# Search steps on PSUM operands, a second raw buffer, and eight gate tiles ahead of attention

## The chip, the cores and the metric

The kernel runs on one core of a Trainium2 chip. The metric is the device time of one launch in microseconds. Engines: PE (TensorE, matrix products), DVE (VectorE), ACT (ScalarE), POOL (GpSimd), and SP, whose queue issues the DMA transfers here.

## What is computed

One layer of a streaming encoder on 1024 prompt frames and 64 sample frames, width 1024, all in float32: a half-step feed-forward block, a block with sparse attention and a convolution in parallel, a second half-step feed-forward block, and a final norm. The middle block, cut to what matters:

```python
z = rms(h) @ w_in                       # q, k, v, q_idx, k_idx, w_idx, conv input, gates
s = einsum('bqhd,bsd->bqhs', q_idx, k_idx)
score = einsum('bqh,bqhs->bqs', w_idx, relu(s))          # -inf beyond the end of the frame's chunk of 64
_, sel = top_k(score, min(256, L // 4))                  # each query keeps its best keys
attn = softmax attention over the selected keys (8 heads, 2 key/value heads)
conv_out = silu(layernorm(depthwise_conv(glu(conv_in)))) @ conv_w_out
g_a, g_c = split(sigmoid(gate + b_gate))
h = h + (g_a * (attn @ attn_w_out) + g_c * conv_out) @ w_out
```

The keys are not gathered: the kernel finds, for each query row, which keys are among the best, and writes a bias row of 0 (keep) or a huge negative number (drop) that is added to the logits.

## The kernel before

Products are in split precision: each float32 operand is cut into a rounded high part and a low remainder, and every product is three matmuls (L154 to L156: high x high, high x low, low x high). Weights come by DMA (L135, `raw<-wf`), ACT makes the high part (L136, `whi`) and POOL the low part (L137, `wlo`).

The order on each engine is not written by hand. The program is traced in Python; a planner with a timeline simulation then orders the instructions of every engine at build time, by priority (a block of code can raise it; otherwise program order) and by when its model thinks operands are ready. On the chip each engine runs its own list strictly in that order. Buffers of a pool with a tag rotate: `bufs` copies exist, and a new use waits until the old one is free. When a pool is closed, later pools reuse its memory and wait for the tiles that lay there.

The stages around the change, in program order:

1. Indexer scores for seven query tiles (`STILES`: six of 128 rows with 384 to 1024 keys, and the sample tile of 64 rows with 192 keys) go into `Y` on DVE (L815). Its last head leaves row sums in `sums`; ACT's square (L817) leaves sums of squares in `cnt`.
2. Value projection, convolution inputs, and the rotated queries `d_q` (L595 to L600). The depthwise convolution runs meanwhile: ACT multiplies (L694, `pd`), POOL adds (L695, `ac`), 30 pairs for each half of a channel tile.
3. The search, all on DVE and with raised priority. Mean and spread of each row give a first threshold (L854 to L867, small steps on [128 x 7] tiles, one column for a query tile). Six rounds then count how many scores reach the threshold (L871, one pass for each query tile), with small steps between (L876 to L888) that move the threshold by a secant rule towards `goal`, top - 3.9. After the last count, L897 drops the counted keys from a copy `F` of the scores, L898 takes the eight largest remaining, `rank` (L891, L893) says how many of them are still needed, L899 and L900 remove these, and L904 writes the bias. L909 to L914 compare what was kept with what should be; if any row is off, a branch runs an exact but long search.
4. K (two groups, `load_k`, L715), V (L927) and the first query tile (`load_q`, L703) are loaded through a staging tile `raw2` in the pool `ak` (L715, L927, L703), and split by ACT (L170, L706) and DVE (L171, L707). `raw2` has one buffer. From the second on, the query tiles lie alternately in the attention pool `ap_`, whose memory follows that of the search's pool.
5. The gate projections: 16 tiles of 128 output columns, each for three column chunks of 362 or 364 frames: 48 groups of 24 matmuls. Each group is evicted by ACT (L942, `sg`) and stored (L943, `d_g`). The first `GPRE` tiles stand ahead of attention, with the four PSUM banks of the pool `ps4`; the others are the start of the "background".
6. Attention over nine query tiles in the order `TORD` = 8, 5, 6, 7, 4, 3, 2, 1, 0, four head pairs for each: logits (L989, L990) into three banks `lg`, bias and maximum on DVE (L992, `mb`), exponential on ACT (L1002), scaling on POOL and DVE (L1006), transposes (L1016) and the product with V. Between slots (pairs of key blocks) it calls the background `FILL[tile]` times; each call advances it by one step: a gate group, a step of the convolution's norm, of its output projection (L1123), of a merge (L1152, L1153) or of the output projection (L1165). A merge of a chunk is not traced before the attention of its frames.
7. The last merge and output projection, and the second feed-forward block.

The other four PSUM banks before attention belong to a pool `lgi`, used by the scores and by one convolution. Attention's pools take over the banks of both.

Of the kernel before, what the change touches and what calls it, by code (L numbers as in the profile page):

```python
# [20 lines left out]
P = 128  # L21
# [25 lines left out]
NLG, NPT = 3, 2  # L47
GPRE = 2
ROUNDS = 6
STOP = float(2 ** 126)  # L50
LOW = -1e36
MS = lambda nc: set()
FILL = {7: 1, 6: 1, 8: 4, 5: 1, 4: 1, 3: 2, 2: 2, 1: 2, 0: 2}
THI = 6000
# [41 lines left out]
def search_table():  # L96

    nd = NormalDist()
    t = np.zeros((P, 14, NT), np.float32)
    for n, (t0, rows, k0, L, top_) in enumerate(STILES):  # L100
        for half in range(2):
            r = slice(64 * half, 64 * half + 64)
            A = L - 64 * (1 - half) * (rows == P)
            z = nd.inv_cdf(1 - (top_ - 4) / A)
            t[r, 0, n], t[r, 1, n] = z, 1 / (A * nd.pdf(z))
        t[:, 2:6, n] = top_ - 3.9, top_, 1 / L, NEG * (L - top_)
    t[:, 6:] = np.tile(np.arange(8), NT).reshape(8, NT)
    return t.reshape(P, -1)


class Kern:
# [342 lines left out]
    def run(self):  # L454
        tc, nc, a = self.tc, self.nc, self.a
        PS = bass.MemoryType.PSUM
        with ExitStack() as top:
# [240 lines left out]
            def load_q(pool, src, t0, rows, qpool=None, qb=2, n=1280):  # L698

                raw = pool.tile([P, n], F32, name="raw2", tag="raw2")[:, 0:1024]  # L700
                raw = raw.rearrange("p (h c) -> p h c", h=8)[:, :, :rows]
                for i in range(4):
                    nc.sync.dma_start(raw[32 * i:32 * i + 32],  # L703
                                      src[i % 2, :, t0:t0 + rows].rearrange("(h r) c -> r h c", r=32))
                qt = (qpool or pool).tile([P, 8, P], F32R, name="qt", tag="qt", bufs=qb)[:, :, :rows]
                nc.scalar.activation(qt, raw, AF.Copy)  # L706
                nc.vector.tensor_tensor(qt[64:], raw[64:], qt[64:], op=ALU.subtract)  # L707
                return qt

            def load_k(pool, r0, name, tmp=None):  # L710
                kh = pool.tile([P, KCOLS], F32R, name=f"kh{name}")
                kl = pool.tile([P, KCOLS], F32R, name=f"kl{name}")
                raw = (tmp or pool).tile([P, 1280], F32, name="raw2", tag="raw2")[:, 0:KCOLS]
                for i in range(4):
                    nc.sync.dma_start(raw[32 * i:32 * i + 32, :], d_k[i % 2, r0:r0 + 32, :])  # L715
                self.split(kh, kl, raw)
                return kh, kl
# [43 lines left out]
            for i in (0, 1):  # L761
# [5 lines left out]
            small = lambda n, w=NT: kp.tile([P, w], F32, name=n)  # L767
            cnt, seen, exc, was, step, slope, gate, thr, unit = (
                small(n) for n in ("cnt", "seen", "exc", "was", "step", "slope", "gate", "thr", "unit"))
            sums = small("sums", 2 * NT)  # L770
            best = kp.tile([P, NT, 8], F32, name="best")
            rank = kp.tile([P, NT, 8], F32, name="rank")
            flags = kp.tile([P, 32], F32, name="flags")
# [9 lines left out]
            nc.sync.dma_start(zt, a["zt"])  # L783
            quant, inv, goal, wanted, per, expect = (zt[:, i * NT:(i + 1) * NT] for i in range(6))

# [10 lines left out]
            for n in SORD:  # L796
# [4 lines left out]
                for hd in range(8):  # L801
                    nb = 2 if L > 512 else 1
                    pw = L // nb
                    for b in range(nb):
# [8 lines left out]
                        else:  # L813
                            kw = {"accum_out": sums[:rows, 2 * n + b:2 * n + b + 1]} if hd == 7 else {}
                            nc.vector.scalar_tensor_tensor(yb, o, wrow[:, hd:hd + 1], yb,  # L815
                                                           op0=ALU.mult, op1=ALU.add, **kw)
                nc.scalar.activation(spare(n), y, AF.Square, accum_out=cnt[:rows, n:n + 1])  # L817
                if rows == P:
# [34 lines left out]
            v = nc.vector  # L853
            v.tensor_tensor(step, sums[:, 0:2 * NT:2], sums[:, 1:2 * NT:2], op=ALU.add)  # L854
            v.tensor_tensor(step, step, per, op=ALU.mult)
            v.tensor_tensor(cnt, cnt, per, op=ALU.mult)
            v.tensor_tensor(slope, step, step, op=ALU.mult)
            v.tensor_tensor(slope, cnt, slope, op=ALU.subtract)
            v.tensor_scalar(exc.bitcast(I32), slope.bitcast(I32), -0.5, 1597463007.0, op0=ALU.mult, op1=ALU.add)
            for i in range(2):  # L860
                v.tensor_tensor(gate, slope, exc, op=ALU.mult)
                v.scalar_tensor_tensor(gate, gate, -0.5, exc, op0=ALU.mult, op1=ALU.mult)
                v.scalar_tensor_tensor(exc, gate, 1.5, exc, op0=ALU.add, op1=ALU.mult)
            v.tensor_tensor(slope, slope, exc, op=ALU.mult)
            v.tensor_tensor(thr, slope, quant, op=ALU.mult)
            v.tensor_tensor(thr, thr, step, op=ALU.add)
            v.tensor_tensor(unit, slope, inv, op=ALU.mult)  # L867
            for r in range(ROUNDS):
                for n in range(NT):
                    rows, y0, L = rows_of(n)  # L870
                    v.tensor_scalar(spare(n), Y[:rows, y0:y0 + L], thr[:rows, n:n + 1], 0.0,  # L871
                                    op0=ALU.is_ge, op1=ALU.add, accum_out=cnt[:rows, n:n + 1])
                if r == ROUNDS - 1:
                    break
                exc, was = was, exc
                v.tensor_tensor(exc, cnt, goal, op=ALU.subtract)  # L876
                v.tensor_tensor(gate, exc, exc, op=ALU.mult)
                if r:
                    v.scalar_tensor_tensor(slope, was, 0.001, exc, op0=ALU.add, op1=ALU.subtract)
                    v.reciprocal(slope, slope)  # L880
                    v.tensor_tensor(slope, slope, step, op=ALU.mult)
                    v.tensor_scalar(slope, slope, 0.25, 4.0, op0=ALU.max, op1=ALU.min)
                    v.tensor_tensor(step, exc, slope, op=ALU.mult)
                else:
                    v.tensor_copy(step, exc)
                v.scalar_tensor_tensor(gate, gate, 16.9, step, op0=ALU.is_gt, op1=ALU.mult)
                v.tensor_tensor(gate, gate, unit, op=ALU.mult)
                v.tensor_tensor(thr, thr, gate, op=ALU.add)  # L888

            v.tensor_tensor(gate, wanted, cnt, op=ALU.subtract)  # L890
            v.tensor_tensor(rank, gate.rearrange("p (n o) -> p n o", o=1).to_broadcast([P, NT, 8]),  # L891
                            zt[:, 6 * NT:].rearrange("p (n o) -> p n o", o=8), op=ALU.is_gt)
            v.tensor_scalar(rank, rank, 2 * STOP, -STOP, op0=ALU.mult, op1=ALU.add)  # L893
            for n in range(NT):
                rows, y0, L = rows_of(n)
                f = F[:rows, y0:y0 + L]
                v.scalar_tensor_tensor(f, spare(n), -STOP, Y[:rows, y0:y0 + L], op0=ALU.mult, op1=ALU.add)  # L897
                v.max(best[:rows, n, :], f)  # L898
                v.tensor_tensor(best[:rows, n, :], best[:rows, n, :], rank[:rows, n, :], op=ALU.min)  # L899
# [25 lines left out]
            vt = ak.tile([P, 2, 10, P], F32R, name="vt")  # L925
            raw = ak.tile([P, 1280], F32, name="raw2", tag="raw2").rearrange("p (b d) -> p b d", d=P)
            nc.sync.dma_start(raw[:, 0:9, :], d_v[:, 0:9, :])  # L927
# [498 lines left out]
```

## Time and profile before

| | us |
|---|---|
| median of 3 runs | 2435.06 (2434.07 to 2438.32) |
| profiled execution | 2435.61 |
| its span | 2433.8 |
| PE busy | 2307.9 (95%) |
| DVE busy | 1677.8 (69%) |
| POOL busy | 1404.1 (58%) |
| ACT busy | 1146.8 (47%) |

The span is the time from the first to the last instruction that the profiler saw; the 1.8 us beside it lie around the program. Rows of the profile name an engine, a line of the kernel, the tile written and the tiles read. A row of waits reads: who waited, for whom, total us, times, longest. A row with a stretch reads: from and to in us, its length, then the busy time and number of instructions of each engine, the granted clock of PE (1.00 is full), the DMA share and GB/s. A row of a line reads: number, then shortest, median and longest duration in ns, first and last start.

### The profile page before, as it was taken

How to read it: one execution, taken by the hardware profiler on the slowest of the kernel's cores; microseconds unless marked ns; L12 is line 12 of the kernel's file. 1: busy time of each engine (PE TensorE's matmuls, PEld its weight loads, DVE VectorE, ACT ScalarE, POOL GpSimd, SP SyncE). 2: the span in 40 equal slices, each digit the busy share in tenths (PEclk: the TensorE clock that was granted, in tenths of full speed). 3: DMA queues.
4: the chain of work that ended last, by engine and by line, in shares of the span. 5: the costliest groups of instructions: out<-in, count | busy, mean ns of one | idle time of the engine just before them, and what ended most of it. 6: DMA issues, size and time to landing. Idle time of an engine off the chain costs nothing.

```text
span 2433.8 us, 43946 instructions
## 1 busy us (share of the span) xinstructions
PE 2307.9 (95%) x16762; PEld 2278.1 (94%) x16762; DVE 1677.8 (69%) x3600; ACT 1146.8 (47%) x2189; POOL 1404.1 (58%) x861
## 2 busy tenths in 40 slices
PE   5999999999999999989699888799999999999998
PEld 5999999999999999989699888799999999999997
DVE  7666678666678386689634897358666677776676
ACT  5434445434346556865554664235443445433343
POOL 4555555555557786888662444457555555555554
PEclk9999999999999999999899999899999999999999
DMA  4222223223224344333223345752232322332223
GB/s 164 96 96 96 93 99 122 98 88 105 96 90 137 126 136 126 95 113 100 63 83 110 102 143 173 261 175 101 87 105 87 100 99 80 110 104 102 96 96 116
DMA packets 130118, 271.92 MB, mean 112 GB/s; under 512 B 18032, under 2 KB 77296, under 8 KB 129904
## 3 DMA queue, kind: packets, MB, share of 16 engines
q1 hardware_dynamic: 129904, 269.08, 33.1%
q8 instruction: 132, 2.16, 0.4%
q14 instruction: 82, 0.67, 0.1%
HBM read 230.34 MB, written 38.75 MB: 111 GB/s over the span
## 4 chain that ended last, share of the span: by engine, by line
PE 40%; DVE 6%; DMA 3%; issue 1%; ACT 1%; POOL 0%; SPq 0%; DVEq 0%; ACTq 0%
PE ps L154 12%; PE ps L156 12%; PE ps L155 12%; DMA ga<-d_g 1%; PE pt L1016 1%; DVE ga L1153 1%; DMA d_mp<-gc 1%; PE lg L989 1%; PE lg L990 0%; PE ps L184 0%; DVE pr L992 0%; PE pv L154 0%; DMA hr<-d_h 0%; DMA gc<-d_g 0%; PE pv L155 0%
## 5 line engine op out<-in xcount | busy, mean ns | idle before, releaser
L137 POOL TENSOR_TENSOR wlo<-raw,whi 128x1024 fp32r<-128x1024 f32 (+1 forms) x187 | 435.4, 2333 | 421.9 <-ACT whi L136 406.7
L154 PE MATMUL ps<-x,wp 128*128 128x272 f32 x1760 | 508.8, 291 | 11.2 <-DVE spare L302 9.2
L156 PE MATMUL ps<-x,wp 128*128 128x272 f32 x1760 | 506.3, 291 | 1.0 <-DVE wp L171 0.4
L155 PE MATMUL ps<-x,wp 128*128 128x272 f32 x1760 | 506.9, 289 | 0.0
L154 PE MATMUL ps<-x,whi 128*128 128x272 f32 (+2 forms) x1544 | 483.2, 313 | 18.2 <-ACT sg L942 8.8
L156 PE MATMUL ps<-x,wlo 128*128 128x272 f32 (+2 forms) x1544 | 481.5, 312 | 0.0
L155 PE MATMUL ps<-x,whi 128*128 128x272 f32 (+2 forms) x1334 | 412.3, 309 | 0.0
L154 PE MATMUL ps<-gh,whi 128*128 128x272 f32 x1408 | 400.0, 289 | 6.8 <-DVE spare L302 5.0
L155 PE MATMUL ps<-gl,whi 128*128 128x272 f32 x1408 | 404.9, 289 | 0.0
L156 PE MATMUL ps<-gh,wlo 128*128 128x272 f32 x1408 | 403.8, 288 | 0.0
L171 POOL TENSOR_TENSOR wlo<-raw,whi 128x1024 fp32r<-128x1024 f32 x88 | 220.1, 2502 | 263.8 <-ACT whi L170 260.6
L154 PEld LDWEIGHTS ps<-x,wp 128*128 128x128 f32 x1760 | 333.1, 189 | 12.2 <-ACT wp L170 12.2
L155 PEld LDWEIGHTS ps<-x,wp 128*128 128x128 f32 x1760 | 333.6, 190 | 0.0
L156 PEld LDWEIGHTS ps<-x,wp 128*128 128x128 f32 x1760 | 331.0, 189 | 2.3 <-DVE wp L171 1.7
L154 PEld LDWEIGHTS ps<-x,whi 128*128 128x128 f32 x1544 | 293.1, 190 | 20.3 <-ACT sg L942 9.3
L171 POOL TENSOR_TENSOR wp<-s,wp 128x512 fp32r<-128x512 f32 x176 | 258.7, 1470 | 90.0 <-ACT wp L170 90.0
L136 ACT ACTIVATE whi<-raw 128x1024 fp32r<-128x1024 f32 (+1 forms) x187 | 190.7, 1020 | 234.8 <-PE ps L155 127.2
L156 PEld LDWEIGHTS ps<-x,wlo 128*128 128x128 f32 x1544 | 292.9, 190 | 1.0
L442 DVE SCALAR_TENSOR_TENSOR h<-ps,h 128x272 f32<-128x272 f32 x384 | 164.7, 439 | 184.7 <-PE ps L156 184.2
L695 POOL TENSOR_TENSOR ac<-ac,pd 128x559 f32<-128x559 f32 x180 | 259.8, 1444 | 45.8 <-ACT pd L694 15.5
L154 PEld LDWEIGHTS ps<-gh,whi 128*128 128x128 f32 x1408 | 263.0, 189 | 8.3 <-DVE spare L302 5.7
L156 PEld LDWEIGHTS ps<-gh,wlo 128*128 128x128 f32 x1408 | 265.8, 189 | 0.0
(236 smaller groups left out, 4815.3 us busy)
## 6 DMA issues: line engine op xcount, KB each, us to landing
raw<-wf SPq DMA_DIRECT2D x334, 512.0 KB, 3.2
raw<-wf SPq DMA_DIRECT2D x32, 384.0 KB, 3.0
d_g<-sg SPq DMA_DIRECT2D x32, 181.0 KB, 1.9
d_h<-h SPq DMA_DIRECT2D x2, 2176.0 KB, 10.4
y<-t SPq DMA_DIRECT2D x32, 136.0 KB, 1.8
raw<-d_q SPq DMA_DIRECT2D x32, 128.0 KB, 2.7
raw<-d_qi SPq DMA_DIRECT2D x24, 128.0 KB, 3.0
d_g<-sg SPq DMA_DIRECT2D x16, 182.0 KB, 2.0
```

What stands on the lines that cost most here:

```text
L136: nc.scalar.activation(hi[:, :n], raw[:, :n], AF.Copy)
L137: self.weng.tensor_tensor(lo[:, :n], raw[:, :n], hi[:, :n], op=ALU.subtract)
L154: t.matmul(out, wh, xh, start=first, stop=False)
L155: t.matmul(out, wh, xl, start=False, stop=False)
L156: t.matmul(out, wl, xh, start=False, stop=last)
L171: (eng or nc.vector).tensor_tensor(lo, x, hi, op=ALU.subtract)
L442: nc.vector.scalar_tensor_tensor(x, p, 0.5, x, op0=ALU.mult, op1=ALU.add)
L695: nc.gpsimd.tensor_tensor(ac, ac, pd, op=ALU.add)
L989: nc.tensor.matmul(o, q, kh[:, ks:ks + pw], start=True, stop=False)
L1016: nc.tensor.transpose(pt[:kn, o:o + r], u.pr[hh][:, kk:kk + kn], ident[:r, :r])
L1153: nc.vector.scalar_tensor_tensor(ga, mpt, 0.5, ga, op0=ALU.mult, op1=ALU.add)
```

## The change

- The search's small tiles: `goal`, `over`, `slope`, `gate`, `cen` and `rank` become slices of one PSUM bank (`bank`, from the pool `lgi`). `goal` is copied there from the table, `exc` is computed a second time as `over` in PSUM, the mean is held twice (`cen` in PSUM, `mean` in SBUF), and a root of its own (`root`) takes the place of `exc` in the square root. Most small steps then read at most one operand from SBUF.
- ACT's square is scaled by L to the power -0.5, so that the step that divided `cnt` goes.
- The rank table holds o - 3.4 rather than o, and is compared with `goal` - `cnt` rather than `wanted` - `cnt`. For whole counts both give the same answer.
- In the last round, count, L897's drop and L898's maximum are done tile by tile, and no longer all counts first.
- `raw2` in the pool `ak` has two buffers.
- `GPRE` is 8 rather than 2, and `FILL[8]` is 2 rather than 4.

```diff
-GPRE = 2
+GPRE = 8
-FILL = {7: 1, 6: 1, 8: 4, 5: 1, 4: 1, 3: 2, 2: 2, 1: 2, 0: 2}
+FILL = {7: 1, 6: 1, 8: 2, 5: 1, 4: 1, 3: 2, 2: 2, 1: 2, 0: 2}
-    t[:, 6:] = np.tile(np.arange(8), NT).reshape(8, NT)
+    t[:, 6:] = np.tile(np.arange(8) - 3.4, NT).reshape(8, NT)
...
-                raw = pool.tile([P, n], F32, name="raw2", tag="raw2")[:, 0:1024]
+                raw = pool.tile([P, n], F32, name="raw2", tag="raw2", bufs=2 if n == 1280 else 1)[:, 0:1024]
-                raw = (tmp or pool).tile([P, 1280], F32, name="raw2", tag="raw2")[:, 0:KCOLS]
+                raw = (tmp or pool).tile([P, 1280], F32, name="raw2", tag="raw2", bufs=1 if tmp else 2)[:, 0:KCOLS]
...
-                nc.scalar.activation(spare(n), y, AF.Square, accum_out=cnt[:rows, n:n + 1])
+                nc.scalar.activation(spare(n), y, AF.Square, scale=L ** -0.5, accum_out=cnt[:rows, n:n + 1])
...
-            v.tensor_tensor(step, sums[:, 0:2 * NT:2], sums[:, 1:2 * NT:2], op=ALU.add)
-            v.tensor_tensor(step, step, per, op=ALU.mult)
-            v.tensor_tensor(cnt, cnt, per, op=ALU.mult)
-            v.tensor_tensor(slope, step, step, op=ALU.mult)
+            bank = lgi.tile([P, 512], F32, name="srch", tag="lgi")
+            goal, over, slope, gate, cen = (bank[:, 16 * i:16 * i + NT] for i in range(5))
+            rank = bank[:, 128:128 + 8 * NT].rearrange("p (n o) -> p n o", o=8)
+            v.tensor_copy(goal, target)
+            v.tensor_tensor(gate, sums[:, 0:2 * NT:2], sums[:, 1:2 * NT:2], op=ALU.add)
+            v.tensor_tensor(cen, gate, per, op=ALU.mult)
+            v.tensor_tensor(mean, gate, per, op=ALU.mult)
+            v.tensor_tensor(slope, cen, mean, op=ALU.mult)
...
+            for r in range(ROUNDS - 1):
+                for n in range(NT):
+                    count(n, spare(n))
                 exc, was = was, exc
+                v.tensor_tensor(over, cnt, goal, op=ALU.subtract)
                 v.tensor_tensor(exc, cnt, goal, op=ALU.subtract)
-                v.tensor_tensor(gate, exc, exc, op=ALU.mult)
+                v.tensor_tensor(gate, exc, over, op=ALU.mult)
                 if r:
-                    v.scalar_tensor_tensor(slope, was, 0.001, exc, op0=ALU.add, op1=ALU.subtract)
+                    v.scalar_tensor_tensor(slope, was, 0.001, over, op0=ALU.add, op1=ALU.subtract)
...
-                    v.tensor_copy(step, exc)
+                    v.tensor_scalar(step, over, 1.0, None, op0=ALU.mult)
...
-            v.tensor_tensor(gate, wanted, cnt, op=ALU.subtract)
+            for n in range(NT):
+                rows, y0, L = rows_of(n)
+                f = F[:rows, y0:y0 + L]
+                count(n, spare(n))
+                v.scalar_tensor_tensor(f, spare(n), -STOP, Y[:rows, y0:y0 + L], op0=ALU.mult, op1=ALU.add)
+                v.max(best[:rows, n, :], f)
+            v.tensor_tensor(gate, goal, cnt, op=ALU.subtract)
...
-                v.scalar_tensor_tensor(f, spare(n), -STOP, Y[:rows, y0:y0 + L], op0=ALU.mult, op1=ALU.add)
-                v.max(best[:rows, n, :], f)
...
-            raw = ak.tile([P, 1280], F32, name="raw2", tag="raw2").rearrange("p (b d) -> p b d", d=P)
+            raw = ak.tile([P, 1280], F32, name="raw2", tag="raw2", bufs=2).rearrange("p (b d) -> p b d", d=P)
```

More of the change, by code (lines that the diff above doesn't have):

```diff
@@ L767, in run @@
             small = lambda n, w=NT: kp.tile([P, w], F32, name=n)
-            cnt, seen, exc, was, step, slope, gate, thr, unit = (
-                small(n) for n in ("cnt", "seen", "exc", "was", "step", "slope", "gate", "thr", "unit"))
+            cnt, seen, exc, was, step, mean, thr, unit, root = (
+                small(n) for n in ("cnt", "seen", "exc", "was", "step", "mean", "thr", "unit", "root"))
             sums = small("sums", 2 * NT)
             best = kp.tile([P, NT, 8], F32, name="best")
-            rank = kp.tile([P, NT, 8], F32, name="rank")
             flags = kp.tile([P, 32], F32, name="flags")
@@ L783, in run @@
             nc.sync.dma_start(zt, a["zt"])
-            quant, inv, goal, wanted, per, expect = (zt[:, i * NT:(i + 1) * NT] for i in range(6))
+            quant, inv, target, wanted, per, expect = (zt[:, i * NT:(i + 1) * NT] for i in range(6))
             def rows_of(n):
@@ L858, in run @@
+            v.tensor_copy(goal, target)
[3 more added lines that the diff above has]
+            v.tensor_tensor(slope, cen, mean, op=ALU.mult)
             v.tensor_tensor(slope, cnt, slope, op=ALU.subtract)
-            v.tensor_scalar(exc.bitcast(I32), slope.bitcast(I32), -0.5, 1597463007.0, op0=ALU.mult, op1=ALU.add)
+            v.tensor_scalar(root.bitcast(I32), slope.bitcast(I32), -0.5, 1597463007.0, op0=ALU.mult, op1=ALU.add)
@@ L860, in run @@
             for i in range(2):
[L861 to L864, printed above, removed]
+                v.tensor_tensor(gate, slope, root, op=ALU.mult)
+                v.scalar_tensor_tensor(gate, gate, -0.5, root, op0=ALU.mult, op1=ALU.mult)
+                v.scalar_tensor_tensor(root, gate, 1.5, root, op0=ALU.add, op1=ALU.mult)
@@ L865, in run, with count @@
+            v.tensor_tensor(slope, slope, root, op=ALU.mult)
             v.tensor_tensor(thr, slope, quant, op=ALU.mult)
-            v.tensor_tensor(thr, thr, step, op=ALU.add)
+            v.tensor_tensor(thr, thr, cen, op=ALU.add)
             v.tensor_tensor(unit, slope, inv, op=ALU.mult)
-            for r in range(ROUNDS):
-                for n in range(NT):
[L870 to L874, printed above, removed]
+            def count(n, out):
+                rows, y0, L = rows_of(n)
+                v.tensor_scalar(out, Y[:rows, y0:y0 + L], thr[:rows, n:n + 1], 0.0,
+                                op0=ALU.is_ge, op1=ALU.add, accum_out=cnt[:rows, n:n + 1])
@@ L888, in run @@
                 v.tensor_tensor(thr, thr, gate, op=ALU.add)
-            v.tensor_tensor(gate, wanted, cnt, op=ALU.subtract)
+            for n in range(NT):
+                rows, y0, L = rows_of(n)
+                f = F[:rows, y0:y0 + L]
[3 more added lines that the diff above has]
+            v.tensor_tensor(gate, goal, cnt, op=ALU.subtract)
             v.tensor_tensor(rank, gate.rearrange("p (n o) -> p n o", o=1).to_broadcast([P, NT, 8]),
```

## The prediction

> **What bounds the kernel now.** I read the profile's page first (shares and the forty slices), then busy time by stretches, then the waits of each engine around the stretch that stood out, then DVE's timeline inside it.
>
> ```profile
> span 2433.8 us, 43946 instructions
> PE 2307.9 (95%) x16762; PEld 2278.1 (94%) x16762; DVE 1677.8 (69%) x3600; ACT 1146.8 (47%) x2189; POOL 1404.1 (58%) x861
> ```
>
> PE is busy for 95% of the span, so a gain is PE idle time removed. The 126 us of it that are idle are not spread evenly:
>
> ```profile
> 1077.00:1088.00 11.00, 2.17 (x12) 1.87 (x11) 10.59 (x33) 5.92 (x8) 3.09 (x3) 0.69 0.71 206
> 1130.00:1153.00 23.00, 23.00 (x141) 23.00 (x140) 22.96 (x29) 10.34 (x15) 18.03 (x12) 1.00 0.35 113
> 1153.00:1174.00 21.00, 0.62 (x4) 0.31 (x3) 13.85 (x48) 0.81 (x1) 0.84 (x1) 0.58 0.00 0
> 1174.00:1320.00 146.00, 145.33 (x940) 140.40 (x940) 68.69 (x173) 83.91 (x163) 88.97 (x50) 0.99 0.27 86
> 1320.00:1487.00 167.00, 152.29 (x1037) 142.07 (x1035) 139.54 (x367) 99.71 (x223) 75.75 (x45) 0.97 0.43 131
> ```
>
> Columns: stretch, length, then busy time of PE, PEld, DVE, ACT, POOL, the granted clock, DMA share, GB/s. The key search runs on DVE from 1057 to 1173. PE covers it with gate projections, but has two holes: about 9 us near 1080 and 20 us before 1174. After 1174 PE is full (145.33 of 146), so time gained there is kept.
>
> ```profile
> PE lg L989 <- DVE mb L992: 21.1, 2, 20.4
> PE ps L154 <- ACT sg L942: 8.8, 1, 8.8
> ACT qt L706 <- DVEq L914: 22.3, 1, 22.3
> ACT kh L170 <- DMA raw<-d_k: 7.2, 1, 7.2
> SPq L703 <- DVE qt L707: 26.9, 1, 26.9
> 1153.10 0.33 PE L156 MATMUL ps<-x,wlo 128*128 128x364 f32 x1
> 1173.81 0.42 PE L989 MATMUL lg<-kh,qt 128*64 128x192 f32 x1 [20.38 <-DVE mb L992]
> L942 ACT ACTIVATE sg<-ps,hb x20: 542/564/567, 1058.9 to 1146.0; 128x362 f32<-128x362 f32 x13, 128x364 f32<-128x364 f32 x7
> ```
>
> (Total, times, longest.) The big hole: PE has a logit matmul next in its queue, waiting for DVE, and DVE is still in the search and its branch (L914). ACT stands 22.3 us at the second query tile's conversion, which waits for that branch, and SP stands 26.9 us behind the only raw buffer. Twenty gate groups were evicted and about two more computed when all stopped: although only two gate tiles (6 groups) stand ahead of attention in the program, the planner had already pulled 22 groups forward. A group is 24 matmuls; at 141 matmuls in 23 us that is 3.9 us, or 4.0 with the 364-frame chunks.
>
> **The change part by part.**
>
> *Small steps on PSUM.* Six stretches hold all small steps from the sums to the last threshold update:
>
> ```profile
> 1057.27:1066.38 9.11, 8.62 (x16) 1.00 0.62 187
> 1073.98:1077.47 3.49, 3.32 (x8) 1.00 0.60 177
> 1084.34:1086.24 1.90, 1.60 (x11) 0.50 0.56 124
> 1095.35:1100.41 5.06, 4.75 (x11) 1.00 0.39 108
> 1107.62:1115.05 7.43, 7.12 (x11) 1.00 0.68 189
> 1120.69:1130.19 9.50, 9.20 (x10) 1.00 0.13 44
> sum 36.49, DVE 34.60; mean DVE 5.77
> 1126.35 0.17 DVE L886 SCALAR_TENSOR_TENSOR gate<-gate,step 128x7 f32<-128x7 f32 x1
> 1126.55 1.25 DVE L887 TENSOR_TENSOR gate<-gate,unit 128x7 f32<-128x7 f32 x1
> 1127.84 2.32 DVE L888 TENSOR_TENSOR thr<-thr,gate 128x7 f32<-128x7 f32 x1
> L207 DVE TENSOR_TENSOR rt<-rv,ps x57: 145/157/159, 11.4 to 2425.1; 128x3 f32<-128x3 f32 x54, 128x4 f32<-128x4 f32 x3
> L208 DVE SCALAR_TENSOR_TENSOR rt<-rt,ps x57: 135/157/159, 11.9 to 2425.3; 128x3 f32<-128x3 f32 x54, 128x4 f32<-128x4 f32 x3
> ```
>
> The third round had POOL idle: ten steps in 1.90 us, 0.19 each. The last round, the same ten steps beside a busy POOL (7 adds and weight splits), took 9.50: 7-column steps of 0.17 become 1.25 or 2.32. The nearest rows with one operand in PSUM are the norm's steps, L207 and L208: 114 of them over the whole span, POOL 58% busy, none above 0.159. So I price every changed step at 0.20. Before there are 16 + 6 + 4x10 = 62 steps; after 17 + 7 + 4x11 = 68 (a copy of the goals, a second centre, `over` in each round; the square's scale removes one). 68 x 0.20 = 13.6 against 36.5. One new step, `gate` from two halves of the sums, still reads SBUF twice: +0.7, its excess now. Search shorter by 22.2 us; bounds 22.9 (no waits at all) and -1.2, that is longer, if PSUM does not help and only the six steps are added.
>
> *Rank table and reordered last round.* The same comparisons of integers with shifted constants, and the same 7 counts, 7 combinations (L897) and 7 maxima, interleaved: no instruction gone. The prices that matter are these:
>
> ```profile
> 1135.74:1148.85 13.11, 13.11 (x81) 13.11 (x80) 13.11 (x11) 6.42 (x10) 11.45 (x6) 1.00 0.37 116
> 1157.76:1165.57 7.81, 0.00 (x0) 0.00 (x0) 7.80 (x22) 0.00 (x0) 0.00 (x0) 0.50 0.00 0
> L904 DVE SCALAR_TENSOR_TENSOR bias<-F,fill x7: 345/814/1210, 1157.8 to 1165.2; 128x384 bf16<-128x384 f32 x1, 128x512 bf16<-128x512 f32 x1, 128x640 bf16<-128x640 f32 x1, 128x768 bf16<-128x768 f32 x1
> 1166.24 0.19 DVE L912 TENSOR_REDUCE flag<-turned 128x1 int32<-128x32 f32 x1
> 1173.40 0.35 DVE L992 CUSTOM_DVE_ANT_0 pr<-lg,bias 64x192 f32<-64x192 f32 x1 [6.98 <-DVEq L914]
> ```
>
> The combinations read two SBUF tiles and took 13.1 us beside a POOL busy for 11.45. The seven masks (L904) have the same shapes and also read two SBUF tiles, but took 0.81 in the middle, 5.6 in all, with POOL at 0.00 (late replacements fill the rest of the 7.81). POOL was idle there only because ACT was stuck and fed it nothing. Once the search ends sooner, some masks fall where POOL still works. From 0 to (13.1 - 5.6) = 7.5 us more; I take 3. The flag and the branch stay at 7 us. The search's end moves from 1173.1 to 1173.1 - 22.2 + 3 = 1153.9.
>
> The Trainium skill has a rule that speaks against this change here: "SBUF — State Buffer", section Who interferes with whom, says a DVE instruction with two SBUF inputs contends with a GpSimd instruction that reads SBUF, and the later one waits in full. By it all seven masks would wait wherever POOL is busy; the L897 row agrees, no run here shows it for masks. The sum by it is the second rival below.
>
> *Second raw buffer.* K's second group could not be loaded until DVE had split the first; ACT stood 7.2 us for it, and the eviction behind it, the sixth, held PE for 8.8:
>
> ```profile
> 1086.99 0.54 ACT L942 ACTIVATE sg<-ps,hb 128x362 f32<-128x362 f32 x1
> 1087.58 0.67 PE L154 MATMUL ps<-x,whi 128*128 128x364 f32 x1 [8.83 <-ACT sg L942]
> ```
>
> With two buffers the load is issued early. The 8.8 us do not add to the gain: without them the other 18 groups run from 1087.58 - 8.83 = 1078.7 and end at 1078.7 + 18 x 3.95 = 1149.8 rather than 1160, in either case near the search's end. Worth 0 to 2 by itself; if the cover (the search) were gone, 8.8. SP's 26.9 us go too; what is late next is the second query conversion, which still waits for the branch.
>
> *Eight gate tiles ahead, FILL[8] 4 to 2.* No matmul, transfer or eviction is added. Ahead of attention must now stand 24 groups, not the 22 that the planner had put there: 2 x 4.0 = 8.0 us of PE work moves into a hole. The price: attention's banks come from the gates' pool, so no logits are computed ahead, and the last evictions and the ninth tile's weights queue on ACT behind the query conversion. I bound this backlog from below by that conversion alone and from above by conversion, weight split, three evictions and some five conv products with POOL's pace:
>
> ```profile
> 1173.19 1.06 ACT L706 ACTIVATE qt<-raw 128x1024 fp32r<-128x1024 f32 x1 [22.33 <-DVEq L914]
> 1174.16 1.04 ACT L136 ACTIVATE whi<-raw 128x1024 fp32r<-128x1024 f32 x1
> 1175.10 0.55 ACT L942 ACTIVATE sg<-ps,hb 128x362 f32<-128x362 f32 x1
> L695 POOL TENSOR_TENSOR ac<-ac,pd x44: 1373/1392/2247, 1118.9 to 1249.4; 128x559 f32<-128x559 f32 x44
> ```
>
> 1 to 1.06 + 1.04 + 3 x 0.55 + 5 x 1.39 = 11 us; I take 6. PE resumes at 1153.9 + 6 = 1160, not 1173.8: 13.8 us.
>
> In the background's list, gates fall from 42 steps to 24; 78 others stay. Fill calls fall from 120 to 112, so ten find nothing, near tile 2, where the merge waits for attention. A conv-out step there is 12 matmuls, 2.0 us; ten make 20. The matmuls are only moved, so this costs PE idle at most: 0 to 20. At the 9% that PE is idle from 1320 to 1487, 2 us.
>
> **Sum.** -13.8 - 8.0 + 2 = -20 us. The profiled execution took 2435.61 (span 2433.8, 1.8 around it), 0.5 above the median of 2435.06. I apply -20 to the median: 2415.
>
> **The rivals.**
>
> 1. *The backlog takes the place of the search.* ACT's order, or the freeing of the gates' banks, holds the first logits 10 us longer than I allow. For: ACT's single 22.3 us wait held everything. Against: the planner puts evictions at PE's pace. -20 + 10: 2425.
> 2. *Masks wait for POOL.* 7.5 in place of 3: 2419.5. For: L897's row. Against: ACT stops feeding POOL when it reaches the query conversion.
> 3. *The steps still wait.* Then the search ends at 1174.3; only the two groups move, less 1.2 and 2 for the fills: -5, 2430. Against: L207, L208.
> 4. *Slower: attention runs out of filler.* Ten empty calls at tile 2, where PE then waits for DVE. At 2.0 us each it leaves 2 us of the gain, 2433; at the 4.0 us of an output-projection step (24 matmuls) it is +40 in place of +2: 2453. It decides from 2.2 us of new idle per empty call. Against: PE was idle for only 14.7 us in the whole of that stretch, and the planner fills from further down.
> 5. *Larger gain.* No mask waits (3), backlog of 1 (5), and the freed SP and the conv that runs on save some 5 more of the 14.7: -33, 2402.
>
> **How the numbers follow.** Chances: forecast 0.50 (its own range 2405 to 2423), rival 1 0.15, 2 0.12, 3 0.04, 4 0.11, 5 0.08. Low: rival 5 less a few us, 2399; high: rival 1 with some of 3, 2429. Rival 4's 0.11 stays mostly outside. About 0.2% (4.9 us) is what a measurement can tell from no change. Faster: 0.50 + 0.12 of rival 1 + 0.12 + 0.02 + 0.08 = 0.84. Same: 0.03 of rival 1, 0.02 of 3, 0.03 of 4 = 0.08. Slower: 0.08 of 4.
>
> **What would show it.** Steps right: none of the PSUM steps above 0.25, six stretches near 14 us in sum. Search: the branch ends near 1154. Gates: 24 evictions before the first logit, and PE's hole at most 12 us. Raw buffer: no wait of ACT for d_k near 1071, none of SP on L707 beyond a few us. Masks: their stretch at 8 to 15. Wrong would be: the hole still 20 us, steps above 1 us, or more than 25 us of PE idle in the 167 us after the dense stretch.

## The result, and the profile after

The changed kernel took 2394.70 us (median of 4 runs, 2393.04 to 2398.54) against 2435.23 for the kernel before (4 runs, 2434.07 to 2438.32): ratio 0.9834, 95% interval 0.9817 to 0.9851. That is 40.5 us where 20 were forecast, and below the range (2399). The profiled execution took 2394.04, its span 2392.3, 41.5 less than before. Lines have moved: the scores L815 are L814 in the changed kernel, the eviction L942 is now L952, the logits L989 and L990 are L999 and L1000, the masks L904 are L914, the flag L912 is L922, the branch L914 is L924, the merge's L1152 is L1162.

The page of the changed kernel, first line of engines:

```profile
PE 2301.7 (96%) x16762; PEld 2272.7 (95%) x16762; DVE 1656.9 (69%) x3606; ACT 1145.4 (48%) x2189; POOL 1410.0 (59%) x861
```

PE idle fell from 125.9 us (2433.8 - 2307.9) to 90.6. The other 6.2 us are busy time: the same 16762 matmuls took less. Where the idle went is read from four stretches. Kernel before:

```profile
1040.00:1160.00 120.00, 104.60 (x628) 103.77 (x626) 112.85 (x218) 64.88 (x102) 95.32 (x62) 0.94 0.34 106
1160.00:1290.00 130.00, 115.51 (x747) 111.48 (x748) 62.94 (x166) 71.28 (x140) 79.06 (x46) 0.94 0.24 76
1290.00:1450.00 160.00, 148.53 (x1002) 138.49 (x1001) 122.50 (x311) 91.46 (x190) 67.77 (x35) 0.98 0.39 119
1450.00:1610.00 160.00, 135.44 (x792) 131.95 (x791) 83.42 (x166) 61.87 (x125) 75.92 (x41) 0.91 0.62 205
```

Changed kernel:

```profile
1040.00:1160.00 120.00, 113.19 (x685) 112.70 (x684) 103.60 (x244) 73.14 (x116) 109.96 (x68) 0.97 0.40 122
1160.00:1290.00 130.00, 130.00 (x843) 126.33 (x842) 53.56 (x140) 69.55 (x136) 73.95 (x44) 1.00 0.27 85
1290.00:1450.00 160.00, 145.62 (x987) 135.49 (x986) 142.22 (x354) 95.31 (x206) 75.90 (x40) 0.97 0.43 131
1450.00:1610.00 160.00, 145.70 (x887) 141.76 (x886) 93.34 (x199) 67.43 (x136) 84.74 (x43) 0.98 0.66 214
```

PE idle (length less PE busy) went from 15.4 to 6.8, from 14.5 to 0, from 11.5 to 14.4 and from 24.6 to 14.3. The first two rows, 23.1 us, hold the two holes that the prediction spoke of (8.8 and 20.4 us before, one of 6.8 now). The last row, 10.3 us, is the stretch of the merges, most of it past 1487, where the prediction's views ended.

Inside the first two rows: the last of the six stretches of small steps with the sum of all six, then the stretch of the masks:

```profile
1105.12:1107.36 2.24, 2.24 (x16) 2.24 (x15) 1.90 (x11) 2.10 (x4) 2.16 (x3) 1.00 0.23 83
sum 13.31, PE 13.31 PEld 13.31 DVE 11.21 ACT 7.71 POOL 11.24; mean PE 2.22 PEld 2.22 DVE 1.87 ACT 1.28 POOL 1.87
```

```profile
1135.52:1149.47 13.95, 13.95 (x86) 13.95 (x85) 13.95 (x22) 6.75 (x10) 11.56 (x7) 1.00 0.41 135
```

The groups of the three steps that were shown before, and of the gate evictions from 1040 to 1160 (busy us, mean ns of one, idle before them):

```profile
L893 DVE TENSOR_TENSOR srch<-srch,unit 128x7 f32<-128x7 f32 x5 | 0.9, 174 | 0.2
L892 DVE SCALAR_TENSOR_TENSOR srch<-srch,step 128x7 f32<-128x7 f32 x5 | 0.9, 173 | 0.2
L894 DVE TENSOR_TENSOR thr<-thr,srch 128x7 f32<-128x7 f32 x5 | 0.8, 163 | 0.2
...
L952 ACT ACTIVATE sg<-ps,hb 128x362 f32<-128x362 f32 (+1 forms) x24 | 13.0, 546 | 0.9 <-PE ps L156 0.9
```

The timelines of DVE, ACT and PE around the search's end (start, length, and in brackets the idle time before):

```profile
1112.94 13.63 DVE L900 SCALAR_TENSOR_TENSOR F<-bias,Y 128x384 f32<-128x384 bf16 x7
...
1149.51 1.24 DVE L919 TENSOR_TENSOR srch<-seen,zt 128x7 f32<-128x7 f32 x1
...
1151.23 0.19 DVE L922 TENSOR_REDUCE flag<-turned 128x1 int32<-128x32 f32 x1
1159.53 0.35 DVE L1002 CUSTOM_DVE_ANT_0 pr<-lg,bias 64x192 f32<-64x192 f32 x1 [8.11 <-DMA d_g<-sg]
...
1150.75 0.76 ACT L694 ACTIVATE pd<-ci,par 128x559 f32<-128x559 f32 x1 [3.60 <-POOL ac L695]
...
1156.69 0.54 ACT L952 ACTIVATE sg<-ps,hb 128x362 f32<-128x362 f32 x1
...
1159.34 1.06 ACT L706 ACTIVATE qt<-raw 128x1024 fp32r<-128x1024 f32 x1 [0.60 <-DMA d_g<-sg]
...
1157.29 0.42 PE L999 MATMUL lg<-kh,qt 128*64 128x192 f32 x1 [6.81 <-ACT sg L952]
```

That 6.81 is the only wait of PE between 1040 and 1240 in the view of the waits.

A step with at most one operand in SBUF takes 0.15 to 0.21 us in every one of the rounds, beside a POOL that is busy for 11.24 of the 13.31 us; the last round took 2.24 where it took 9.50. The new order of the last round did not reach the chip: seven counts still come first, then the seven drops (L900, 13.63 us where they took 13.11), then the seven maxima, since the planner grouped them. The one small step that still reads two SBUF tiles there (L919) took 1.24. The masks took 13.95, not 7.81: POOL is now busy under them (11.56). PE's last gate matmul ends near 1150.5, but the logits' banks are free only after the last eviction, at 1156.69: on ACT the last two evictions stand behind convolution products and a weight split, and the products wait for POOL's additions. The second query's conversion comes behind the evictions, at 1159.34. All 24 gate groups are evicted ahead of the first logits, and PE resumes at 1157.29 instead of 1173.81.

### The profile page after: what moved, and what is told of

Read it like the earlier page. It is cut to its first block, busy times and chain, and to the rows that moved or that the text cites. A ratio compares the mean times of both kernels' runs of the same rounds, so it can differ in the third digit from the quotient of the medians.

```text
span 2392.3 us, 43957 instructions
## 1 busy us (share of the span) xinstructions
PE 2301.7 (96%) x16762; PEld 2272.7 (95%) x16762; DVE 1656.9 (69%) x3606; ACT 1145.4 (48%) x2189; POOL 1410.0 (59%) x861
## 4 chain that ended last, share of the span: by engine, by line
PE 80%; DVE 9%; DMA 4%; POOL 3%; issue 2%; ACT 2%; SPq 0%; ACTq 0%; DVEq 0%; POOLq 0%
PE ps L154 25%; PE ps L156 25%; PE ps L155 25%; POOL ac L695 2%; DMA ga<-d_g 1%; PE pt L1026 1%; PE ps L184 1%; PE lgi L806 1%; PE lgi L807 1%; DMA d_h<-hr 1%; DVE t L229 1%; DVE ps L330 1%; DVE xl L171 0%; PE lg L999 0%; DVE ps L326 0%
## 5 line engine op out<-in xcount | busy, mean ns | idle before, releaser
L695 POOL TENSOR_TENSOR ac<-ac,pd 128x559 f32<-128x559 f32 x180 | 263.3, 1463 | 32.4 <-ACT ac L690 10.8
L155 PEld LDWEIGHTS ps<-gl,whi 128*128 128x128 f32 x1408 | 265.6, 189 | 0.0
## 6 DMA issues: line engine op xcount, KB each, us to landing
d_h<-h SPq DMA_DIRECT2D x2, 2176.0 KB, 10.5
```

Of the source, the lines that this page charges most:

```text
L155: t.matmul(out, wh, xl, start=False, stop=False)
L695: nc.gpsimd.tensor_tensor(ac, ac, pd, op=ALU.add)
```

## The experiments

Each kernel ran beside the kernel before on the same chip (its medians there: 2433.87 to 2436.93); ratios are to that.

### Taking one part out of the changed kernel

**The search as before, on SBUF** (`a_sbuf_search`): the search's lines of the kernel before; eight gate tiles, FILL[8] 2 and two raw buffers stay.

> The changed kernel with the whole search as it was before (all small tiles in SBUF, old order of the last round); eight gate tiles, FILL[8] 2 and two raw buffers stay. Theory 1 (about 24 us of the gain arise up to the first logits, 14 of them from the shorter search and the rest from two more gate groups; about 17 us arise later, because the background runs ten calls ahead of attention): the search ends near 1173 again, PE resumes there, so 14 to 18 us above the changed kernel's 2395, that is 2409 to 2413. Rival (the later 17 us come from the second raw buffer, which frees SP and lets query tiles come early): the same here, 2409 to 2413. If the small steps were not what shortened the search: 2395.

2412.06 (ratio 0.9895, 0.9878 to 0.9911). PE's and ACT's waits between 1040 and 1240:

```profile
PE lg L989 <- DVE mb L992: 14.1, 1, 14.1
PE lg L989 <- ACT sg L942: 8.1, 1, 8.1
ACT qt L706 <- DVEq L914: 20.1, 1, 20.1
```

PE's waits sum to 22.2 us rather than 6.8, so the search's edits are worth 17 us here (15 by the ratios), 15.4 of them in the hole. The run takes out all of these edits together. That the operands in PSUM are what counts follows from the trace: the order of the last round is the same in both, and the small steps are what became shorter.

**One raw buffer** (`b_one_raw`):

```diff
-name="raw2", tag="raw2", bufs=2
+name="raw2", tag="raw2", bufs=1
```

> The changed kernel with one raw buffer in attention again. Theory 1 (lead of the background): the search is the last to end either way, so 0 to 3 us above 2395; ACT waits for the second K load again, but PE has four banks and hides most of it. Rival (raw buffer carries the later gain): about 17 us above, 2412, with SP held for over 20 us at a query load.

2405.48 (0.9874, 0.9852 to 0.9895): 10.8 above the changed kernel, where 0 to 3 was expected (10 by the ratios).

```profile
PE lg L999 <- ACT sg L952: 19.7, 1, 19.7
ACT qt L706 <- DVEq L924: 13.2, 1, 13.2
```

ACT stands at the second query's conversion, which waits for the branch, and the last gate evictions are behind it in ACT's list; PE cannot start the logits until they free a bank. With two buffers the planner put the conversion behind the last eviction, ACT does not wait for the branch, and PE's wait is 6.8.

**Ten empty steps in the background** (`d_lead0`), which take back the lead that 112 fill calls have over 102 steps:

```diff
+                for _ in range(10):
+                    yield
```

> The changed kernel with ten empty background steps put between the last gate group and the convolution's norm, so that the background's later work stands in the program where it stood before, in relation to attention. Nothing else differs. Theory 1 (lead): up to the last gate the same, then the 17 us are lost: 2408 to 2412, last merge and output projection of the background after attention's end. Rival (raw buffer, or an earlier convolution on POOL): 2395, within 3.

2406.74 (0.9885, 0.9868 to 0.9902): the lead is worth 12 us, with the same hole at the search's end. Stretches as above:

```profile
1040.00:1160.00 120.00, 113.50 (x684) 113.00 (x683) 104.05 (x247) 74.19 (x117) 108.17 (x66) 0.97 0.41 125
1160.00:1290.00 130.00, 130.00 (x849) 126.10 (x848) 52.48 (x139) 68.89 (x133) 72.73 (x42) 1.00 0.29 91
1450.00:1610.00 160.00, 135.73 (x816) 131.74 (x815) 81.35 (x175) 60.33 (x118) 79.21 (x39) 0.95 0.65 207
```

Nothing changed before 1290; PE idle in the merges is 24.3 again, as in the kernel before (24.6), against 14.3.

**Two gate tiles ahead** (`c_gates2`: GPRE 2, FILL[8] 4), and the same with attention's pools `psa` and `psf` in the other order (`f_gates2_swap`), which gives the background other banks:

> The changed kernel with two gate tiles ahead and FILL[8] 4 again; search on PSUM and two raw buffers stay. Theory 1: the shorter search is kept, the two extra groups (8 us) and the lead of ten calls (17 us) are gone: 2415 to 2420. Rival (raw buffer): only the 8 us are gone: 2403.

> Two gate tiles ahead and FILL[8] 4, with search on PSUM and two raw buffers, as in the run that gave 2475; only two lines swapped: attention's transpose banks are taken before the background's two banks, so that the background's banks are no longer one of those the search's small tiles occupy. Bank theory (the seventh or eighth gate group waited 57 us for the bank that holds the search's tiles): that wait is gone, groups are pulled ahead as before, 2412 to 2420. Rival (the order on ACT or PE, not the bank): 2475.

2475.32 (1.0167, 1.0150 to 1.0184) and 2471.93 (1.0161, 1.0134 to 1.0189): both slower than before, and some 50 us above what the theories gave. The rival of the second had the time (2475), but for another reason than the one below. PE's longest wait in the first and in the second, from the view of the waits, and the matmul that waited in the first, from the timeline:

```profile
PE ps L154 <- DVE flags L920: 57.4, 1, 57.4
PE ps L154 <- DVE flags L920: 57.2, 1, 57.2
```

```profile
1142.53 0.67 PE L154 MATMUL ps<-x,whi 128*128 128x364 f32 x1 [57.40 <-DVE flags L920]
```

The search now holds a PSUM tile of the pool `lgi`, and background gates use pools that follow `lgi`. They waited for the search's last use of that tile, and other banks for the background did not help.

### The search's bank in a pool of its own

`i_own_bank` takes the search's tile from a pool `srp` of one bank, with three banks left in `lgi`, two gate tiles ahead and FILL[8] 4; `j_own_bank_lead` is the same with FILL[8] 7 (a lead of 12 calls), `l_own_after` the same with eight tiles and FILL[8] 2.

```diff
-            lgi = self.pool(ps_es, "lgi", 4, space=PS)
+            lgi = self.pool(ps_es, "lgi", 3, space=PS)
+            srp = self.pool(ps_es, "srp", 1, space=PS)
-            bank = lgi.tile([P, 512], F32, name="srch", tag="lgi")
+            bank = srp.tile([P, 512], F32, name="srch", tag="srch")
```

> The changed kernel with two gate tiles ahead and FILL[8] 4 again, as in c_gates2, but the search's PSUM bank in a pool of its own (one bank, the eighth), and three banks left in the scores' pool. Theory: a pool is given back as a whole, so in c_gates2 and f_gates2_swap every background gate waited for the last step on the search's bank, whichever bank the gate itself used. With a pool that only attention's last product overlaps, PE's wait of 57 us for the search's flags goes, gates run under the search as before the change, and with no lead the time is 2400 to 2415. Rival: the gates wait for something else that ends with the search (SBUF of the search's pool); then the wait stays and the time is 2465 to 2480. If three score banks are too few, PE or DVE shows new waits on lgi before 1057 us and up to 10 us more.

> As i_own_bank, but FILL[8] 7, so that the background has a lead of 12 calls over attention rather than none. Theory (lead worth some 10 us, two gate tiles ahead enough once the search has its own pool): 2388 to 2402, about 10 below i_own_bank. Rival (in the changed kernel the eight tiles are what matters, not the lead): no lower than i_own_bank less 3.

> The changed kernel as it is (eight gate tiles, FILL[8] 2) with the search's bank in a pool of its own and three banks for the scores. In it the background starts after the search in any case, so the theory of the pool gives no gain: 2391 to 2399, the same as the changed kernel, unless the fourth score bank is missed (then 2 to 10 more).

2428.25 (0.9970, 0.9955 to 0.9985), 2410.11 (0.9897, 0.9866 to 0.9927) and 2411.91 (0.9888, 0.9853 to 0.9922). The 57 us wait is gone, so it was the pool. Yet the three are 13, 8 and 13 us above the top of what was expected. The scores, with three banks, end later: their last row started at 1084.1, 1084.9 and 1092.0 rather than 1057.0, and the search with it. The scores' line, first in the changed kernel, then in `l_own_after` (shortest, median and longest ns, first and last start):

```profile
L814 DVE SCALAR_TENSOR_TENSOR Y<-lgi,wq,Y x77: 403/619/753, 932.0 to 1057.0; 128x512 f32<-128x512 f32 x21, 128x384 f32<-128x384 f32 x21, 128x448 f32<-128x448 f32 x14, 128x320 f32<-128x320 f32 x14
```

```profile
L815 DVE SCALAR_TENSOR_TENSOR Y<-lgi,wq,Y x77: 408/619/753, 935.5 to 1092.0; 128x512 f32<-128x512 f32 x21, 128x384 f32<-128x384 f32 x21, 128x448 f32<-128x448 f32 x14, 128x320 f32<-128x320 f32 x14
```

The same three with four banks in `lgi` and three in `ps4`: `n_ps3` (two tiles, FILL[8] 4), `m_ps3_lead` (two tiles, FILL[8] 7) and `o_ps3_after` (eight tiles, FILL[8] 2).

> As m_ps3_lead with FILL[8] 4, no lead. Theory (a lead of ten to twelve calls is worth 10 to 18): 2402 to 2416, 10 to 18 above m_ps3_lead. Rival (the lead matters only with eight tiles ahead): the same as m_ps3_lead within 4.

> Two gate tiles ahead, FILL[8] 7 (lead 12), the search's bank in a pool of its own as in j_own_bank_lead, but with all four score banks kept and three banks rather than four for the pool ps4. Theory (what the eight tiles did was only to go round the held pool; the 30 us that j_own_bank_lead lost at the search's start came from the third score bank): the search ends near 1151, PE resumes by 1160, and the time is 2388 to 2400, like the changed kernel. Rival (eight tiles in front of attention are worth something in themselves, since attention's first tile then has the gates' weights and evictions out of its way): 2405 to 2415.

> The changed kernel with eight gate tiles and FILL[8] 2, the search's bank in a pool of its own, four score banks and three banks in ps4. The gates, all in ps4, now have three banks: a group takes 3.95 us on PE and its eviction 0.55 on ACT, so three should do. Theory: 2391 to 2399, the same as the changed kernel, which says that l_own_after's 17 us were the score bank. Rival (the pool of its own costs by another way, the planner's order): 2405 to 2413 as l_own_after.

2422.40 (0.9935, 0.9915 to 0.9956), 2399.43 (0.9856, 0.9830 to 0.9882) and 2393.92 (0.9831, 0.9806 to 0.9855). In all three the last row of scores starts at 1054.0 or before. So the fourth score bank was what `l_own_after` and `j_own_bank_lead` missed (18 and 11 us). For `i_own_bank` it explains 6 us: `n_ps3` is still 6 above the top of its range. `m_ps3_lead` against `n_ps3` is worth 23 us (19 by the ratios), more than expected, but it is not the lead alone: 13.0 us of it are PE idle in the merges (1450 to 1610), and 7.6 lie before 1160, where PE's wait of 10.5 us at the first logits of `n_ps3` is gone. `m_ps3_lead` is 4.7 us above the changed kernel and 5.5 above `o_ps3_after`, which has the same pools; the intervals overlap. So with the pool out of the way and a lead given otherwise, eight tiles ahead are worth some 5 us at most, and that is not shown.

### One part alone in the kernel before

`e_before_lead` has FILL[8] 7 (lead 12), `k_before_two_raw` the second raw buffer, `p_before_gates8` GPRE 8 and FILL[8] 2.

> The kernel before with one number changed: FILL[8] 7 rather than 4, so 132 fill calls for 120 background steps, and the background's later work stands twelve calls earlier in relation to attention. Search, raw buffer and gates ahead are those of before. Theory 1 (the lead by itself is worth what ten empty steps took away, 10 to 12 us): 2424 to 2427, PE idle less in the merge stretch at 1490 to 1640, nothing changed before 1174. Rival (lead pays only together with the earlier search, as attention must not starve): 2435 or slower.

> The kernel before with the second raw buffer alone. My prediction priced the buffer at 0 to 2 by itself: 2433 to 2435, with ACT's 7.2 us wait for d_k and PE's 8.8 us wait for an eviction gone and the 20 us hole at the search's end about 9 us longer. Rival (as taking it out of the changed kernel cost 10): 2424 to 2428.

> The kernel before with GPRE 8 and FILL[8] 2 alone: search in SBUF, one raw buffer. Theory (the lead of ten calls is worth 10 to 12, two more groups go into the hole at the search's end for up to 8, and one raw buffer with this order costs up to 10): 2413 to 2425. My prediction's terms would give 2435 - 8 + 2 + 0 to 6: 2429 to 2435.

The lead: 2423.44 (0.9950, 0.9935 to 0.9966), as expected. The raw buffer: 2442.91 (1.0024, 1.0011 to 1.0036), a loss of some 6 us where 0 to 2 of gain were expected. The gates: 2416.56 (0.9920, 0.9895 to 0.9945), a gain of 19 us, in the expected range and at least three times what the prediction's terms give. Stretches of `p_before_gates8`, and from its waits the one at the first logits:

```profile
1040.00:1160.00 120.00, 108.59 (x661) 108.10 (x659) 112.82 (x220) 64.56 (x102) 95.24 (x60) 0.97 0.36 111
1160.00:1290.00 130.00, 110.30 (x705) 106.93 (x706) 50.32 (x134) 66.21 (x126) 71.91 (x44) 0.91 0.25 79
1450.00:1610.00 160.00, 146.72 (x905) 143.15 (x904) 93.09 (x201) 70.28 (x148) 86.65 (x46) 0.97 0.64 208
```

```profile
PE lg L989 <- ACT sg L942: 31.1, 1, 31.1
```

Up to 1290 PE did 218.9 us of work, 1.2 less than before: the two more groups did not fill the hole, which grew to 31.1. The gain is all later: 13.3 us idle in the merges against 24.6. These 11.3 us are most of it; the profiled execution was the slowest of its four and 15.3 us shorter in span.

### What the lead does

`s_lead0_bufs` is `d_lead0` with four buffers rather than two for the merge's tiles:

```diff
-tag="ga", bufs=2)   ...   tag="mpt", bufs=2)
+tag="ga", bufs=4)   ...   tag="mpt", bufs=4)
```

> d_lead0 (the changed kernel with the lead taken out by ten empty steps) with four buffers rather than two for the merge's ga and mpt. In d_lead0 PE waits 15.7 us once for a merge's gate tile, whose load stands behind the three loads of h (1.45 MB each). Theory (without the lead the last merge steps run with no attention left to cover their loads, and h's loads delay these): with four buffers the gate tiles are asked for earlier, the 15.7 us wait shrinks to a few us, and the time falls from 2407 to 2394 to 2401. Rival (the merges are limited by something else, such as PE's own order): 2403 to 2410, with a PE wait of 10 us or more left in that stage.

2395.55 (0.9845, 0.9828 to 0.9861): 11 us back (10 by the ratios), without the lead. PE's waits for a merge's gate tile between 1450 and 1620, in the kernel before, in the changed one, in `d_lead0` and in `s_lead0_bufs` (total, times, longest):

```profile
PE ps L154 <- DVE ga L1152: 14.6, 6, 6.7
PE ps L154 <- DVE ga L1162: 3.5, 4, 1.3
PE ps L154 <- DVE ga L1162: 16.8, 4, 15.7
PE ps L154 <- DVE ga L1162: 9.5, 3, 8.1
```

The timeline of `d_lead0` on DVE, PE and SP's queue:

```profile
1543.06 0.98 DVE L1162 SCALAR_TENSOR_TENSOR ga<-ga,ps 128x362 f32<-128x362 f32 x2 [15.62 <-DMA ga<-d_g]
1543.65 0.67 PE L154 MATMUL ps<-ah,whi 128*128 128x362 f32 x1 [15.74 <-DVE ga L1162]
1524.18 5.90 SPq L1254 DMA_DIRECT2D h<-d_h  x3
1534.11 1.67 SPq L1157 DMA_DIRECT2D ga<-d_g  x2
```

The merges are short of data, not of matmuls: a merge step needs a gate tile, and in `d_lead0` two of these were asked for 10 us after the three loads of `h` (1.45 MB each). The longest PE wait halved with four buffers; a few us were expected. Whether the loads of `h` took the bandwidth or SP's place in the queue is not told apart, since the planner also issued them 9 us later in `s_lead0_bufs`. Attention is what covers the merges: the last logits start at 1486.8 in the kernel before, at 1521.0 in the changed one, and at 1486.3 in `d_lead0` (the line of the logits in these three, in this order):

```profile
L990 PE MATMUL lg<-kl,qt x104: 249/342/447, 1108.3 to 1486.8; 128*128 128x384 f32 x24, 128*128 128x512 f32 x24, 128*128 128x448 f32 x16, 128*128 128x320 f32 x16
```

```profile
L1000 PE MATMUL lg<-kl,qt x104: 225/338/402, 1157.5 to 1521.0; 128*128 128x384 f32 x24, 128*128 128x512 f32 x24, 128*128 128x448 f32 x16, 128*128 128x320 f32 x16
```

```profile
L1000 PE MATMUL lg<-kl,qt x104: 219/339/628, 1153.9 to 1486.3; 128*128 128x384 f32 x24, 128*128 128x512 f32 x24, 128*128 128x448 f32 x16, 128*128 128x320 f32 x16
```

A longer lead is not better: `g_fill4` is the changed kernel with FILL[8] 4, a lead of 18.

> The changed kernel with FILL[8] 4: 120 fill calls for 102 background steps, a lead of 18 rather than 10. Theory 1: the merge stretch, where PE is still idle 14 us of 160, gets a little more cover: 2388 to 2395; beyond that the background runs into attention not yet done and the calls find nothing. Rival (lead is already used up): 2395, within 2.

2401.19 (0.9869, 0.9841 to 0.9898), 6 above the changed kernel rather than below; the intervals overlap, but the expected gain is not there. PE idle in the merges is 18.8 us, against 14.3 with a lead of 10.

### The masks, and a faster version

`h_fill_psum` copies the masks' constant into the search's bank; `r_ps3_fill` is `o_ps3_after` with the same edit.

```diff
+            fillp = bank[:, 80:81]
+            v.tensor_copy(fillp, fill)
-                ... 10 * LOW, fill[:rows].to_broadcast([rows, L]),
+                ... 10 * LOW, fillp[:rows].to_broadcast([rows, L]),
```

> The changed kernel with the masks' constant read from the search's PSUM bank (one copy more), so that a mask reads one SBUF tile. If masks wait for POOL because they read SBUF twice, their stretch falls from 13.95 us to about 7.8 and the branch ends 5 to 6 us earlier. PE then waits for ACT's last eviction only: theory 1 gives 2392 to 2395; if the search's end alone set PE's restart: 2389.

> o_ps3_after (the changed kernel with the search's bank in a pool of its own, three banks for the gates) and the constant of the masks in PSUM as in h_fill_psum: a try at a version faster than the changed kernel. Masks free: the search ends some 6 us earlier; but PE's wait at the first logits is down to 3 us in o_ps3_after, so at most 3 us can come of it: 2387 to 2395. If PE is the limit by then: the same as o_ps3_after, 2392 to 2395.

2392.57 (0.9830, 0.9805 to 0.9854) and 2387.69 (0.9820, 0.9797 to 0.9842). The masks of `h_fill_psum` take again what they took before beside an idle POOL, though POOL is busy for 6.04 of the 7.50 us from 1137.2 on (their line, then PE's wait at the logits):

```profile
L916 DVE SCALAR_TENSOR_TENSOR bias<-F,srch x7: 340/805/1206, 1137.2 to 1144.6; 128x384 bf16<-128x384 f32 x1, 128x512 bf16<-128x512 f32 x1, 128x640 bf16<-128x640 f32 x1, 128x768 bf16<-128x768 f32 x1
```

```profile
PE lg L1001 <- ACT sg L954: 5.0, 1, 5.0
```

But PE's wait at the logits is for ACT and falls only from 6.8 to 5.0. The second has the lowest median of all, but its interval overlaps that of the changed kernel: faster than before for certain, faster than the changed kernel not shown.

## Why the prediction was wrong, point by point

**What bounds the kernel.** Right in kind: the gain is PE idle removed. Wrong in where it was looked for. The views stopped at 1487, and as much idle time as in the search's large hole lay behind it: 22.8 of the 153 us from 1487 to 1640 in the kernel before (stretch, then busy time of each engine).

```profile
1487.00:1640.00 153.00, 130.17 (x735) 127.10 (x735) 74.00 (x128) 51.25 (x88) 73.36 (x34) 0.92 0.64 211
```

**Small steps.** Right: 14.3 forecast (13.6 + 0.7), 14.2 measured (13.31 and 0.90 for the one step that reads two SBUF tiles). In the whole, `a_sbuf_search` gives 15 to 17 us.

**Masks.** Rival 2, of 0.12, came true: +6.1 us, where 3 was taken. With two SBUF inputs their median was 1.87 us, and five of the seven waited; POOL had run dry when that of 896 keys began, and it and the next took 1.07 and 1.21. In `h_fill_psum`, with one of the two inputs in PSUM, the median was 0.81 beside a POOL that is busy too. It cost little, because PE waited for ACT by then. The Trainium skill, "SBUF — State Buffer", section Who interferes with whom, says that a DVE instruction with two SBUF inputs contends with a GpSimd instruction that reads SBUF. Both runs agree.

**Search's end and PE's resumption.** The flag came 15.0 us earlier, not 19.2, and the first logits are masked at 1159.5. PE resumed at 1157.3; 1160 was forecast. The number is near by luck, for the route was another: ACT's last eviction released PE, 0.8 us before the search's branch was over (1158.1; 1153.9 was forecast). The 6 us of backlog were counted from the search's end, with the evictions behind the query conversion. In the run they stand ahead of it, behind convolution products at POOL's pace, which that step had among its terms; the 6.8 us that PE waits begin at its last gate matmul.

**Raw buffer.** Mis-sized. In the kernel before, the buffer alone cost 6 us (`k_before_two_raw`): the 8.8 us wait went, and as the step says nothing came of it, since PE then waited 33.2 us at its first logits, 21.1 before. In the changed kernel the same buffer is worth 10 to 11 us (`b_one_raw`), but not by the 8.8 us that the step kept for a case without cover: that wait is absent in `b_one_raw` too. It is worth them because, with one buffer, the second query's conversion stands ahead of the last evictions and waits for the branch. The step left that conversion as a wait that stays. With one buffer PE's wait is 19.7, which is rival 1 with a size near its own.

**Two more groups, 8.0 us.** Not shown as a term of its own: with the gate part alone the hole grew, and PE did no more work up to 1290. With all parts together the first two stretches gained 23.1 us of idle, where the terms gave 21.8.

**The step that failed: "At the 9% that PE is idle from 1320 to 1487, 2 us."** The ten fill calls that find nothing were priced as a loss, 0 to 20 us, on the picture that attention needs the background as filler; rival 4 is the same picture. The background's steps wait for data at their end, and need attention as cover. A background that runs ten calls ahead brings merges into attention's reach: `d_lead0` gives 12 us and `e_before_lead` 13. In the stretch of the merges alone PE idle falls by 13.0 from `n_ps3` to `m_ps3_lead`, and by 11.3 in `p_before_gates8`, which gains nothing before it. With -12 in place of +2 the sum is -13.8 - 8.0 - 12 = -33.8, or 2401, inside the range. The 7 us left over are not placed: the busy time that fell by 6.2, which no step priced, is about as large, and its cause stays open.

**Rival 5** (2402) had the direction, for other reasons: the masks took 6.1 us more, not 0. The kernel came out faster, to which 0.84 was given; the range ended 4 us too high.

## What to carry to other kernels

When a change shifts one stream of work against another, follow both to the end of the shorter one: what runs alone there may wait for its loads, and then a lead is worth what a price per moved instruction never shows. A small tile put into PSUM holds its pool until its last use, and a planner that had pulled later work over that stage can do so no longer: give it a pool of its own, and don't take the bank from the stage that sets its start. A part that is worth nothing alone (here a buffer) can be worth 10 us beside others, so price it there as well.

## What the runs showed of the hardware

A hole in PE costs more than its length. After the 15.7 us wait in `d_lead0`, matmuls of one shape start 0.30 us apart, and later 0.17:

```profile
1544.12 0.51 PE L155 MATMUL ps<-al,whi 128*128 128x362 f32 x1
1544.42 0.51 PE L156 MATMUL ps<-ah,wlo 128*128 128x362 f32 x1
...
1549.85 0.33 PE L156 MATMUL ps<-ah,wlo 128*128 128x362 f32 x1
1550.02 0.33 PE L154 MATMUL ps<-ah,whi 128*128 128x362 f32 x1
```

The slow pace lasts from 1543.65 to 1549.85, 6.2 us, in which 20 matmuls start. At 0.166 us they would have taken 3.3, so this hole cost 2.9 us more than its length. The slow pace is shorter elsewhere: 3.9 and 3.1 us after the waits of 8.83 and 20.38 us in the kernel before, and 3.4 after the one of 6.81 in the changed kernel. The Trainium skill, "TensorE: Matmul & The Clock Gate", Part 1 on the clock gate, says that after an idle window the array runs at half rate until it has been busy for about 3.4 us. Three of these four stretches agree in kind and about in length; the one in `d_lead0` is nearly twice as long.

The granted clock of the stretch of the merges was 0.91 before and 0.98 after, and busy time over the whole fell by 6.2 us with no matmul removed. That this comes from fewer holes is not shown. `d_lead0` speaks against it: PE idle in its merges is that of the kernel before, and its PE is busy for 2301.7 us as in the changed kernel.
